# A hybrid encoder layer: the recurrence's first chunks take their product banks from the sweeps' and memory's set instead of the convolution's

## The chip, the cores and the metric

The kernel runs on one core of a Trainium2 chip. The metric is device time in microseconds (us) of one execution; the time before is the median of three runs. Engines: PE = TensorE, DVE = VectorE, ACT = ScalarE, POOL = GpSimd, SP = SyncE (here only a queue that issues DMAs).

## The reference

One encoder layer over 2048 rows of width 1024, fp32. What matters here:

```python
u = _rms_norm(h, norm_mix_g);  proj = u @ w_in
y_hy = _group_rms_norm(_hyena(...))            # convolution over the whole length, by rFFT
y_ml = _group_rms_norm(_mlstm_bidirectional(q, k, v, o_pre, gates, gate_b))  # 4 heads x 128
h = h + concatenate([y_hy, y_ml]) @ w_out
h = h + _cross_attention(_rms_norm(h), _rms_norm(mem), wq, wk, wv, wo)       # 256 memory rows
h = h + square(relu(_rms_norm(h) @ ff_w1)) @ ff_w2
```

The mLSTM is a linear recurrence with gates, computed chunk by chunk:

```python
s = einsum('bhtd,bhsd->bhts', qc, kc) * w                       # scores of the chunk
num = einsum('bhts,bhse->bhte', s, vc) + inter * einsum('bhtd,bhde->bhte', qc, C)
C_new = carry_decay * C + einsum('bhs,bhsd,bhse->bhde', we, kc, vc)
```

It runs forwards and backwards, and the two are summed.

## The kernel before

The kernel works through stages: the input projection ("sweeps"), the long convolution (`hyena`, in steps of PE products at L173 and L186), the gates and the backward states of the recurrence (`states`), a projection of the memory rows (`memproj`), the recurrence (`mlstm`, 16 chunks of 128 rows), the attention with its gemms (L355, L358, L359 are the three partial products of one fp32 product), and the feed-forward part. Neighbouring stages are written interleaved. A scheduler then sets the order of the instructions on each engine from its own estimate of when each can start; so where a tile lives, and what must be free before it can be written, changes the order.

PE writes its products into PSUM. PSUM is eight banks of 128 x 512 fp32 and is divided here in two sets of four: `mm()` gives a bank of the first set (sweeps, memory projection, attention gemms), `hy()` one of the second (convolution, states, recurrence, the attention's transposes). The names `mm<-` and `hy<-` in the rows of the profile tell the set. A bank is given again when everything that reads it is done.

`memproj` goes through eight groups: `project` (L708, 16 products with weights `wm`, then a copy on ACT at L710), and for each of them either `keys` (L725, 16 products in four banks, groups 0 to 3) or `values` (L737, 8 products in four banks, groups 4 to 7). Each bank is copied on ACT (L715) to a tile `o`, which a DMA issued by POOL (L727 `gd<-o`, L739 `vw<-o`) writes to memory.

One chunk of `mlstm` is, on PE: four products `kk_t` by `qn` into one bank (`scores`, L1284); for each of the two directions, eight products in two banks (L1322 from the scores and `va`, L1324 from the state `cf` forwards or `cbn` backwards); and four products in two banks for the new state (`update`, L1200). Chunk 0 has no forward state and so no L1324 in its first direction. Between them POOL and ACT prepare the weights `rw` (L1290, L1291, L1293), DVE multiplies them with the scores (L1294) and brings rows by shuffles (L1275), ACT or DVE divides and reads the two banks (L1327, L1330, L1331; forwards ACT at L1336, backwards DVE at L1338), and DVE forms the state (L1206). After each second chunk `bank_rsqrt` (L208 to L216) computes 13 small operations in one bank, DVE scales the rows (L1356), and a DMA of POOL writes them to `ym`. The scores of chunk n + 1 are written ahead of the products of chunk n.

A step of the convolution does its products into two banks, then L1051 (DVE), L1060 (POOL), L1062 (DVE), `bank_rsqrt` in a third bank, L1064 (DVE), L1066 (POOL), and four DMAs `yh<-a` (L1068). The attention begins by loading rows of `yh` (L1473), turning them on PE (`turn`, L1479) and splitting them (L366) for the first gemm L355.

SP's queue loads everything else: weights `wm` (L415), convolution operands `a<-zg` and `a<-hy` (L339, L974), and the chunks' `qn`, `kk_t`, `cbn`, `va`, `kn`, `og`.

The code around the change, in the program's order: `for _ in chain(p.turned_in(), take(n, 1), beside_each(n, take(m, 5))): pass`, where n is `memproj` and m is `mlstm`: one step of the memory projection, then the remaining steps and the first steps of the recurrence in turn.

Of the kernel before, what the change touches and what calls it, by code (L numbers as in the profile page):

```python
# [128 lines left out]
class Prog:  # L129
    def __init__(self, ctx, tc, a):  # L130
        self.tc, self.nc, self.a = tc, tc.nc, a
        nc = self.nc
        self.ctx = ctx
        self.dr = ctx.enter_context(tc.tile_pool(name="dr", bufs=1, space=DRAM))
        self.s = {}
        cp = self.cp = ctx.enter_context(tc.tile_pool(name="cp", bufs=1))
        ident = cp.tile([128, 128], F32, name="ident")
        nc.gpsimd.memset(ident, 1.0)
        nc.gpsimd.affine_select(ident, ident, pattern=[[-1, 128]], compare_op=ALU.is_equal, fill=0.0,
                                base=0, channel_multiplier=1)  # L140
        self.ident = ident
        self.eps = cp.tile([128, 1], F32, name="eps")
        nc.vector.memset(self.eps, EPS)
        self.ones = cp.tile([128, 128], F32, name="ones")
        nc.vector.memset(self.ones, 1.0)
        self.flip = 0
        self.banks, self.strict = [], False
        self.pending = []
        self.prepq = None
        self.hooks, self.made, self.lag, self.rowb = {}, 0, [], None  # L150
        self.rbp = cp.tile([128, 16], F32, name="rbp")
        self.fb = cp.tile([128, 8], F32, name="fb")
        nc.scalar.activation(self.fb[:, 4:5], self.eps, AF.Copy)
        par = self.par = cp.tile([128, 192], F32, name="par")
        nc.scalar.dma_start(out=par, in_=a["par"])
        self.g_mix, self.g_mem, self.gx, self.gf = (par[:, 8 * i:8 * i + 8] for i in range(4))
        self.cw = par[:, 32:92].rearrange("p (i c) -> p i c", i=3)
        self.cb, self.gb = par[:, 92:112], par[:, 112:128]
        self.ps = ctx.enter_context(tc.tile_pool(name="ps", bufs=1, space=PSUM))
# [4 lines left out]
    def hy(self):  # L164
        t = self.ps.tile([128, 512], F32, tag="hy", name="hy", bufs=4)
        self.banks.append(t[:, 0:1].tensor.name)
        return t

    def beside(self, *products, pin=False):
        names = [p[0].tensor.name for p in products]  # L170
# [31 lines left out]
        else:  # L202
            self.nc.vector.tensor_copy(out, in_)

    def bank_rsqrt(self, pool, ss, n):
        nc, c = self.nc, ss.shape[1]
        m, ys = (pool.tile([128, c], F32, tag="br" + x, name="br" + x, bufs=2) for x in "my")
        nc.scalar.activation(m, ss, AF.Identity, bias=self.eps, scale=1.0 / n)  # L208
        b = self.hy()
        y, t = b[:, 0:c], b[:, 16:16 + c]  # L210
        nc.vector.tensor_scalar(y.bitcast(I32), m.bitcast(I32), -0.5, float(0x5F3759DF), ALU.mult, ALU.add)
        for _ in range(3):
            nc.vector.tensor_copy(ys, y)
            nc.vector.tensor_tensor(t, y, ys, ALU.mult)
            nc.vector.scalar_tensor_tensor(t, t, -0.5, m, ALU.mult, ALU.mult)
            nc.vector.scalar_tensor_tensor(y, t, 1.5, ys, ALU.add, ALU.mult)  # L216
        return y
# [970 lines left out]
    def update(self, sb, new, old, kk, va, r, eng, pin=None, bufs=2):  # L1188
        nc, pin = self.nc, pin or (lambda i: i)
        WC, DC = self.gcols[:, 2], self.gcols[:, 3]  # L1190
        ve = sb.tile([128, 4, 129], F32, tag="ve", name="ve", bufs=bufs) if bufs > 1 else va
        if eng is nc.scalar:
            for h in range(4):
                eng.activation(ve[:, h], va[:, h], AF.Copy, scale=WC[:, r + h:r + h + 1])
        else:
            eng.tensor_tensor(ve, va, WC[:, r:r + 4].unsqueeze(2).broadcast_to([128, 4, 129]), ALU.mult)
        for p in range(2):
            pc = self.hy()
            for i in range(2):
                pin(nc.tensor.matmul(pc[:, 129 * i:129 * i + 129], kk[:, 2 * p + i], ve[:, 2 * p + i], start=True, stop=True))  # L1200
            if old is None:
                nc.vector.tensor_copy(new[:, 2 * p:2 * p + 2].rearrange("d h e -> d (h e)"), pc[:, 0:258])
                continue
            for i in range(2):
                h = 2 * p + i
                nc.vector.scalar_tensor_tensor(new[:, h], old[:, h], DC[:, r + h:r + h + 1],  # L1206
                                               pc[:, 129 * i:129 * i + 129], ALU.mult, ALU.add)
# [19 lines left out]
    def mlstm(self, es):  # L1227
# [51 lines left out]

        def scores(n, ld):  # L1280
            qn, kk_t, cbn, va, rows_ = ld
            sp = self.hy().rearrange("p (h t) -> p h t", h=4)
            for h in range(4):
                nc.tensor.matmul(sp[:, h], kk_t[:, h], qn[:, h], start=True, stop=True)  # L1284
            for d in range(2):
                r = 64 * d + 4 * n
                nm = rows_[d, 0]
                if (d, 1) in rows_:
                    it = rows_[d, 1]
                    nc.gpsimd.tensor_tensor(it, it, qn, ALU.mult)  # L1290
                nc.gpsimd.tensor_tensor(nm, nm, masks[d].unsqueeze(1).broadcast_to([128, 4, 128]), ALU.add)  # L1291
                for h in range(4):
                    nc.scalar.activation(nm[:, h], nm[:, h], AF.Exp, bias=GC[:, r + h:r + h + 1])  # L1293
                nc.vector.tensor_tensor(nm, nm, sp, ALU.mult)  # L1294
# [4 lines left out]
        for n in range(16):  # L1299
# [10 lines left out]
            for d in range(2):  # L1310
                r = 64 * d + 4 * n
                nm = rows_[d, 0]
                state = cf if d == 0 else cbn
                if d == 0:
                    y = sb.tile([128, 4, 128], F32, tag="h0", name="ht", bufs=2)
                pvs = []
                for p in range(2):
                    pn = self.hy()
                    for i in range(2):
                        h = 2 * p + i  # L1320
                        dst = pn[:, 129 * i:129 * i + 129]
                        nc.tensor.matmul(dst, nm[:, h], va[:, h], start=True, stop=state is None)  # L1322
                        if state is not None:
                            nc.tensor.matmul(dst, rows_[d, 1][:, h], state[:, h], start=False, stop=True)  # L1324
                    pvs.append(pn[:, 0:258].rearrange("t (h e) -> t h e", h=2))
                for p, pv in enumerate(pvs):
                    nc.scalar.activation(pn[:, 260 + 2 * p:262 + 2 * p].unsqueeze(2), pv[:, :, 128:129], AF.Abs)  # L1327
                den = sb.tile([128, 4, 1], F32, tag="den", name="den", bufs=4)
                dv = den.rearrange("t h o -> t (h o)")
                nc.vector.tensor_tensor(dv, pn[:, 260:264], EC[:, r:r + 4], ALU.max)  # L1330
                nc.vector.reciprocal(dv, dv)  # L1331
                for p, pv in enumerate(pvs):
                    for i in range(2):
                        h = 2 * p + i
                        if d == 0:
                            nc.scalar.activation(y[:, h], pv[:, i, 0:128], AF.Copy, scale=dv[:, h:h + 1])  # L1336
                            continue
                        nc.vector.scalar_tensor_tensor(y[:, h], pv[:, i, 0:128], dv[:, h:h + 1], y[:, h], ALU.mult, ALU.add)  # L1338
# [10 lines left out]
                nc.scalar.activation(junk[:, h], y[:, h], AF.Square, accum_out=ss[:, c:c + 1])  # L1349
            ys.append(y)  # L1350
            if n % 2:
                rv = self.bank_rsqrt(sb, ss, 128)
                for i, y in enumerate(ys):
                    t0 = 128 * (n - 1 + i)
                    for h in range(4):
                        nc.vector.scalar_tensor_tensor(y[:, h], y[:, h], rv[:, 4 * i + h:4 * i + h + 1],  # L1356
                                                       gml[:, 128 * h:128 * h + 128], ALU.mult, ALU.mult)
                    stores.append(lambda t0=t0, y=y: nc.gpsimd.dma_start(
                        out=ym[t0:t0 + 128].rearrange("t (h e) -> t h e", h=4), in_=y))
# [717 lines left out]
def chain(*gens):  # L2077
    for g in gens:
        yield from g
# [20 lines left out]
def program(p):  # L2100
    with ExitStack() as ms:
        with ExitStack() as es:
# [13 lines left out]
            n = p.memproj()  # L2116
            m = p.mlstm(ms)
            with ExitStack() as hs:
# [4 lines left out]
                             among(chain(p.sweep((6, 7), 0, False), p.natural(0, (2,), p.prep_mem, 2)), back, 1),  # L2123
                             )
                weave(rest, p.hyena(hs), 445, 329)
            for _ in chain(p.turned_in(), take(n, 1), beside_each(n, take(m, 5))):
                pass
        with ExitStack() as rs:
            p.ts = rs.enter_context(ExitStack())
            p.tail_open(p.ts)  # L2130
# [71 lines left out]
```

## Time and profile before

| what | value |
|---|---|
| time, median of 3 runs | 3063.18 us (3056.71 to 3065.72) |
| time of the profiled execution | 3063.97 us |
| its span, first to last instruction | 3062.3 us |
| mean granted TensorE clock | 0.989 |
| PE busy | 97% of the span |
| memory projection's last product ends, first attention product L355 starts | 1131.7 us, 1170.91 us |

In the profile's views "x8" counts records, of which PE leaves two for most products; an idle time in square brackets is what the engine waited just before the row, with the instruction or transfer that ended it. "PEclk" is the granted clock as a share of full speed, and the DMA share is the mean busy share of the core's 16 DMA engines.

### The profile page before, as it was taken

The numbers are of one execution on the slowest core, as the hardware profiler recorded it, in microseconds if no ns is written. First come the engines' busy times: TensorE is split into PE (matmuls) and PEld (weight loads), VectorE is DVE, ScalarE is ACT, GpSimd is POOL, SyncE is SP. The second block draws the span as 40 slices with busy tenths as digits, with TensorE's granted clock in tenths as the row PEclk, the third lists the DMA queues.
The fourth block names the chain that finished last, engine by engine and source line by source line (L and its number), as shares of the span: only waits on it lengthen the run. The fifth ranks groups of instructions, "written<-read, shape, count | busy, mean of one in ns | idle before, by whom it ended". The sixth has DMA issues, their size and how long they took to land.

```text
span 3062.3 us, 44144 instructions
## 1 busy us (share of the span) xinstructions
PE 2979.0 (97%) x14799; PEld 2367.6 (77%) x14799; DVE 1953.2 (64%) x3442; ACT 1491.5 (49%) x2930; POOL 1263.4 (41%) x1025
## 2 busy tenths in 40 slices
PE   9999999998999989999999999999999999999998
PEld 7666667775678867888888888888888888888876
DVE  8855464557755447867665666558555686566695
ACT  6443455634664235555544455556555543333335
POOL 0112113321443654333223247765665374344653
PEclk9999999999999999999999999999999999999999
DMA  6655676686877976463567466657544555444434
GB/s 223 197 186 170 213 263 214 192 273 216 279 229 221 348 265 198 149 228 125 196 202 264 137 219 217 208 178 250 190 151 152 196 192 169 118 157 121 155 103 165
DMA packets 423644, 607.03 MB, mean 198 GB/s; under 512 B 36847, under 2 KB 229999, under 8 KB 422393
## 3 DMA queue, kind: packets, MB, share of 16 engines
q1 hardware_dynamic: 395972, 525.42, 53.6%
q0 software_dynamic: 18992, 62.96, 5.6%
q10 hardware_dynamic: 8452, 15.83, 1.4%
q8 instruction: 117, 1.92, 0.3%
q14 instruction: 111, 0.90, 0.1%
HBM read 401.67 MB, written 202.41 MB: 197 GB/s over the span
## 4 chain that ended last, share of the span: by engine, by line
PE 58%; DVE 2%; DMA 1%; issue 1%; ACT 1%; POOL 0%; SPq 0%; DVEq 0%; POOLq 0%; ACTq 0%
PE mm L355 12%; PE mm L359 12%; PE mm L358 12%; PE hy L355 6%; PE hy L359 6%; PE hy L358 6%; PE hy L1322 1%; PE hy L1324 1%; DVE bl L1693 0%; PE hy L1284 0%; PE hy L1596 0%; DVE acc L1991 0%; PE hy L1200 0%; PE hy L1479 0%; DVE acc L2028 0%
## 5 line engine op out<-in xcount | busy, mean ns | idle before, releaser
L1692 ACT CAST ah<-w 128x512 fp32r<-128x512 f32 x284 | 176.6, 623 | 303.8 <-PE hy L358 150.2
L1693 DVE TENSOR_TENSOR bl<-wr,bh 128x512 fp32r<-128x512 f32 x213 | 240.3, 1132 | 126.5 <-ACT bh L1692 126.2
L366 DVE TENSOR_TENSOR wl<-wn,wh 128x512 fp32r<-128x512 f32 (+1 forms) x296 | 220.0, 787 | 89.2 <-ACT wh L366 89.2
L355 PE MATMUL mm<-xh,wh 128*128 128x512 f32 x640 | 264.5, 415 | 2.3 <-ACT xh L366 1.1
L358 PE MATMUL mm<-xl,wh 128*128 128x512 f32 x640 | 255.9, 400 | 5.5 <-DVE xl L366 5.4
L359 PE MATMUL mm<-xh,wl 128*128 128x512 f32 x640 | 254.5, 398 | 0.0
L1692 ACT CAST bh<-wr 128x512 fp32r<-128x512 f32 x232 | 143.4, 621 | 227.9 <-PE mm L359 169.5
L1693 DVE TENSOR_TENSOR al<-w,ah 128x512 fp32r<-128x512 f32 x236 | 216.5, 918 | 57.2 <-ACT ah L1692 56.9
L359 PE MATMUL mm<-bh,al 128*128 128x512 f32 x576 | 223.8, 391 | 3.4 <-DVE al L1693 3.4
L355 PE MATMUL mm<-bh,ah 128*128 128x512 f32 x576 | 225.9, 392 | 1.3 <-DVE acc L1854 1.1
L358 PE MATMUL mm<-bl,ah 128*128 128x512 f32 x576 | 224.9, 390 | 0.0
L366 ACT CAST wh<-wn 128x512 fp32r<-128x512 f32 (+1 forms) x296 | 164.3, 620 | 102.6 <-PE mm L359 51.1
L358 PE MATMUL mm<-act,wh 128*128 128x512 f32 x512 | 202.0, 395 | 0.0
L359 PE MATMUL mm<-act,wl 128*128 128x512 f32 x512 | 199.9, 392 | 0.0
L355 PE MATMUL mm<-act,wh 128*128 128x512 f32 x512 | 199.0, 395 | 0.6 <-ACT wh L366 0.5
L355 PE MATMUL hy<-bh,ah 128*128 128x512 f32 x448 | 175.2, 391 | 0.0
L358 PE MATMUL hy<-bl,ah 128*128 128x512 f32 x448 | 174.6, 390 | 0.0
L359 PE MATMUL hy<-bh,al 128*128 128x512 f32 x448 | 174.4, 390 | 0.0
L331 POOL TENSOR_TENSOR b<-b 128x512 f32<-128x512 f32 x32 | 48.1, 1504 | 293.6 <-DVE b L330 277.4
L355 PEld LDWEIGHTS mm<-xh,wh 128*128 128x128 f32 x640 | 121.1, 190 | 52.4 <-issue 18.7
L358 PEld LDWEIGHTS mm<-xl,wh 128*128 128x128 f32 x640 | 121.2, 189 | 50.9 <-issue 19.1
L355 PE MATMUL mm<-wh,xh 128*128 128x256 f32 (+1 forms) x512 | 155.7, 304 | 1.8 <-DVE a L960 1.8
(396 smaller groups left out, 8257.4 us busy)
## 6 DMA issues: line engine op xcount, KB each, us to landing
wr<-hc SPq DMA_DIRECT2D x224, 256.0 KB
w<-in_ff_w_dram SPq DMA_DIRECT2D x172, 256.0 KB
hc<-wn SPq DMA_DIRECT2D x128, 256.0 KB
wn<-in_w_in_dram SPq DMA_DIRECT2D x100, 256.0 KB
hc<-q SPq DMA_DIRECT2D x96, 256.0 KB
fs<-a SPq DMA_DIRECT2D x32, 512.0 KB
zs<-a POOLq DMA_DIRECT2D x32, 512.0 KB, 6.6
a<-fs SPq DMA_DIRECT2D x64, 256.0 KB
```

Source lines behind the costliest of these rows:

```text
L331: nc.gpsimd.tensor_tensor(b, f, b, ALU.subtract)
L355: first = mm(ps, lh, rh, start=start, stop=False)
L358: mm(ps, lh, rl, start=False, stop=False)
L359: self.last = mm(ps, ll, rh, start=False, stop=stop)
L366: both = (self.nc.scalar.copy(hi, src), self.nc.vector.tensor_tensor(lo, src, hi.bitcast(F32), ALU.subtract))
L1322: nc.tensor.matmul(dst, nm[:, h], va[:, h], start=True, stop=state is None)
L1324: nc.tensor.matmul(dst, rows_[d, 1][:, h], state[:, h], start=False, stop=True)
L1692: self.nc.scalar.copy(hi, src)
L1693: eng.tensor_tensor(lo, src, hi.bitcast(F32), ALU.subtract)
```

## The change

A method `spare()` gives a bank of the first set while a flag `early` is set, and of the second otherwise. Scores, chunk products, the state's product and the bank of the chunk's `bank_rsqrt` call it. The flag is set only around the loop in which the memory projection and the first chunks of the recurrence are written. Chunks written later, beside the attention, take `hy()` as before; so do the backward states and the convolution, which are written earlier.

```diff
+        self.early = False
...
+    def spare(self):
+        return self.mm() if self.early else self.hy()
...
-    def bank_rsqrt(self, pool, ss, n):
+    def bank_rsqrt(self, pool, ss, n, bank=None):
...
-        b = self.hy()
+        b = bank or self.hy()
...
         for p in range(2):                       # update
-            pc = self.hy()
+            pc = self.spare()
...
-            sp = self.hy().rearrange("p (h t) -> p h t", h=4)
+            sp = self.spare().rearrange("p (h t) -> p h t", h=4)
...
                 for p in range(2):               # a chunk's direction
-                    pn = self.hy()
+                    pn = self.spare()
...
-                rv = self.bank_rsqrt(sb, ss, 128)
+                rv = self.bank_rsqrt(sb, ss, 128, self.spare())
...
+            p.early = True
             for _ in chain(p.turned_in(), take(n, 1), beside_each(n, take(m, 5))):
                 pass
+            p.early = False
```

Both kernels issue the same number of instructions on every engine. The order differs on PE between about 1024 and 1184 us of the profile, and on the other engines in the same place; before and behind it the two orders are the same. In the rows below a number such as x16 counts instructions. The line numbers of the changed kernel are four higher than the profile's from L177 on (L1288 is L1284, L1326 and L1328 are L1322 and L1324, L1204 is L1200, L712 is L708, L729 is L725, L741 is L737, L1483 is L1479, L359 is L355, L177 and L190 are L173 and L186).

On PE in the kernel before, the end of the memory projection: the last products of its values groups, then chunk 2 (first rows only).

```order
L1324 MATMUL hy<-cbn,rw 128x129
L737 MATMUL mm<-wm,kt 128x512 x3
L1200 MATMUL hy<-ve,kn 128x129 x4
L1284 MATMUL hy<-qn,kk_t 128x128 x4
L1322 MATMUL hy<-va,rw 128x129
L1324 MATMUL hy<-cf,rw 128x129
```

Behind these rows come the rest of chunk 2, the whole of chunk 3, the 16 transposes of L1479, half a direction of chunk 4 and then the first L355, with no other product between.

On PE in the changed kernel, the same end.

```order
L1204 MATMUL mm<-ve,kn 128x129 x4
L712 MATMUL mm<-mt,wm 128x256 x16
L741 MATMUL mm<-wm,kt 128x512 x8
L712 MATMUL mm<-mt,wm 128x256 x16
L741 MATMUL mm<-wm,kt 128x512 x16
L1483 MATMUL hy<-ident,wn 128x128 x16
L1288 MATMUL hy<-qn,kk_t 128x128 x4
L1326 MATMUL hy<-va,rw 128x129
L1328 MATMUL hy<-cf,rw 128x129
```

The first row is the end of chunk 3; after it the last three groups of the projection stand without a chunk between, and the transposes and chunk 4 follow the last L741 at once.

On PE in the changed kernel, chunk 0 and the convolution steps around it, in the second and third group of the keys.

```order
L729 MATMUL mm<-kt,wm 128x256 x12
L1288 MATMUL mm<-qn,kk_t 128x128 x4
L1326 MATMUL mm<-va,rw 128x129 x5
L1204 MATMUL hy<-va,kn 128x129 x4
L1326 MATMUL mm<-va,rw 128x129
L1204 MATMUL mm<-ve,kn 128x129 x4
L712 MATMUL mm<-mt,wm 128x256 x13
L177 MATMUL hy<-a,e_2743 32x512
L190 MATMUL hy<-a,e_2743 32x512 x7
L712 MATMUL mm<-mt,wm 128x256 x3
```

Before, at this place stood only L708, L725 and convolution steps; chunk 0's L1284 came behind the last convolution step. Row 4 is a backward state of the recurrence, which keeps its `hy` bank.

On PE in the changed kernel, the last two convolution steps, after the products of chunk 1.

```order
L1328 MATMUL mm<-cbn,rw 128x129
L177 MATMUL hy<-a,e_2743 32x512
L190 MATMUL hy<-a,e_2743 32x512 x7
L1204 MATMUL mm<-ve,kn 128x129 x4
L177 MATMUL hy<-a,e_2743 32x512
L190 MATMUL hy<-a,e_2743 32x512 x7
L712 MATMUL mm<-mt,wm 128x256 x16
```

Before, at least 19 products of L708 and L725 or L737 lay between two steps of the convolution; here four L1204 lie between the last two.

## The prediction

> **What bounds the kernel now.** I read the page's busy table first, then the windows around the code that the change touches, then PE's own timeline there, then the timelines of DVE and SP. The page:
>
> ```profile
> PE 2979.0 (97%) x14799; PEld 2367.6 (77%) x14799; DVE 1953.2 (64%) x3442; ACT 1491.5 (49%) x2930; POOL 1263.4 (41%) x1025
> ```
>
> PE sets the time: 97% busy, so only what changes PE's own idle or slow time can move the end. The change adds and removes no instruction; it moves rows of about 1024 to 1184 us. These windows (length, busy time of PE, PEld, DVE, ACT, POOL, then granted clock, DMA share, GB/s) show that piece:
>
> ```profile
> 1025.00:1045.00 20.00, 20.00 (x109) 16.74 (x108) 9.88 (x31) 3.72 (x7) 11.05 (x13) 1.00 1.04 386
> 1065.00:1085.00 20.00, 20.00 (x91) 14.19 (x91) 11.33 (x33) 4.61 (x9) 15.12 (x19) 1.00 1.04 353
> 1085.00:1105.00 20.00, 20.00 (x90) 13.16 (x89) 6.07 (x17) 4.30 (x8) 12.40 (x15) 1.00 0.83 315
> 1105.00:1131.50 26.50, 26.50 (x132) 18.43 (x131) 13.72 (x38) 14.13 (x49) 15.09 (x18) 1.00 0.71 222
> 1131.50:1171.00 39.50, 23.39 (x138) 21.39 (x136) 26.16 (x98) 22.64 (x88) 19.23 (x18) 0.74 0.58 186
> ```
>
> Up to 1131.5 (the memory projection) PE is full at full clock, with the DMA engines full too until 1085. The last row, a tail between the memory projection and the first attention product, is the slow place: PE is idle for 16 of 39.5 us and the clock is 0.74. PE's timeline there (start, duration, instructions in a row, then the idle time before them and what ended it):
>
> ```profile
> 1128.97 2.74 PE L737 MATMUL mm<-wm,kt 128*128 128x512 f32 x6
> 1134.20 1.13 PE L1284 MATMUL hy<-qn,kk_t 128*128 128x128 f32 x8 [1.60 <-issue]
> 1142.23 0.77 PE L1322 MATMUL hy<-va,rw 128*128 128x129 f32 x2 [5.12 <-DVE bry L213]
> 1145.10 0.80 PE L1322 MATMUL hy<-va,rw 128*128 128x129 f32 x2 [0.81 <-DVE ht L1356]
> 1149.31 2.09 PE L1200 MATMUL hy<-ve,kn 128*128 128x129 f32 x8 [2.12 <-ACT ht L1336]
> 1151.19 1.92 PE L1284 MATMUL hy<-qn,kk_t 128*128 128x128 f32 x8
> 1156.51 0.39 PE L1322 MATMUL hy<-va,rw 128*128 128x129 f32 x2
> 1156.73 0.39 PE L1324 MATMUL hy<-cbn,rw 128*128 128x129 f32 x2
> 1157.48 1.23 PE L1200 MATMUL hy<-ve,kn 128*128 128x129 f32 x8 [0.36 <-ACT ht L1336]
> 1159.41 0.66 PE L1479 MATMUL hy<-ident,wn 128*128 128x128 f32 x4 [0.70 <-DVE cf L1206]
> 1160.38 1.29 PE L1479 MATMUL hy<-ident,wn 128*128 128x128 f32 x8 [0.32 <-issue]
> 1166.72 1.12 PE L1479 MATMUL hy<-ident,wn 128*128 128x128 f32 x4 [5.04 <-DVE act L366]
> 1170.91 1.18 PE L355 MATMUL mm<-act,wh 128*128 128x512 f32 x4
> ```
>
> L1284, L1322/L1324 and L1200 are one chunk of the recurrence. Chunks 2 and 3 run here alone: each step waits for DVE or ACT, with no other product between. The idle times add up to 16.07 us. The same instructions take twice as long after a wait (L1284 1.92 against 1.05 at full clock, row below; L1200 2.09 against 1.06), so part of the busy time is lost too.
>
> **What the change does to it.** The pieces of order above show it: chunks 0 to 3 move from the end of the memory projection to between its product groups (chunk 0 behind keys 1, chunk 1 behind keys 2, chunk 2 behind keys 3, chunk 3 behind values 0), since a score or a chunk product no longer waits for a convolution bank. After the last L737 follow the transposes of L1479, chunk 4 and L355.
>
> Count from 1024.22, where the first row differs, to the first L355 at 1170.91: 146.7 us. PE's work between is the same in both kernels. These are rows for its rates:
>
> ```profile
> 1020.70 3.68 PE L725 MATMUL mm<-kt,wm 128*128 128x256 f32 x8 [2.36 <-ACT kt L710]
> 1024.22 4.91 PE L708 MATMUL mm<-mt,wm 128*128 128x256 f32 x22
> 1047.94 1.89 PE L725 MATMUL mm<-kt,wm 128*128 128x256 f32 x8
> 1063.07 0.61 PE L173 MATMUL hy<-a,e 64*32 64x512 f32 x1
> 1073.35 0.61 PE L173 MATMUL hy<-a,e 64*32 64x512 f32 x1
> 1086.18 0.61 PE L173 MATMUL hy<-a,e 64*32 64x512 f32 x1
> 1121.93 1.05 PE L1284 MATMUL hy<-qn,kk_t 128*128 128x128 f32 x8
> 1131.54 1.06 PE L1200 MATMUL hy<-ve,kn 128*128 128x129 f32 x8
> ```
>
> Removed, first term. The tail holds three groups each of L1284 and L1200 (0.9 us from start to start at full clock), 36 products of L1322/L1324 (0.22 apart, as at 1156.51 and 1156.73) and 16 of L1479 (0.16): 5.4 + 8.0 + 2.6 = 16.0 us at full rate. It takes 39.4, of which 16.1 are idle, so 7.3 are lost to the clock. Full-rate work from 1024.22 is 146.7 - 16.1 - 7.3 = 123.3 us: if the new order never waited, the gain would be 23.4 us.
>
> Added, second term: what stays bare at the end. In before, the load of the hyena rows for L1479 waits for the last L737 (it takes over memory of the weights) and hides under chunks 2 and 3:
>
> ```profile
> 1131.77 0.81 SPq L1473 DMA_DIRECT2D wn<-yh  x2
> ym<-ht POOLq DMA_DIRECT2D x2, 256.0 KB, 2.3
> gd<-o POOLq DMA_DIRECT2D x16, 256.0 KB, 7.5
> ```
>
> Its rule stays, and now nothing stands between. The trace does not show this load's own landing; the landings beside it run from 2.3 to 7.5 us. I take 3, near the lower, as the projection's transfers are over by then. The 5.04 wait of the fourth transpose should go: it was for DVE's splits, queued behind a chunk's normalisation, which will be past. Bounds: 2 to 10 with that wait back.
>
> Added, third term: waits inside the projection. A chunk holds two banks for a direction's products until ACT (L1336) or DVE (L1338) has read them, and one bank for its scores. All of these now come from the same four banks that L708, L725 and L737 need, so a chunk can hold up projection products and the other way round. These DVE rows price one convolution step between two products (L1051 to L1064), which runs on the same engine in order:
>
> ```profile
> 1064.19 1.29 DVE L1051 TENSOR_TENSOR a<-hy,a 128x512 f32<-128x512 f32 x2 [4.41 <-PE hy L186]
> 1067.49 1.22 DVE L1062 TENSOR_REDUCE ms<-a 128x16 f32<-128x1024 f32 x1 [2.01 <-POOL a L1060]
> 1071.87 1.22 DVE L1064 TENSOR_TENSOR a<-a,hy 128x1024 f32<-128x1024 f32 x1
> 1144.97 0.72 DVE L1275 STREAM_SHUFFLE rw<-rows 128x512 f32<-128x512 f32 x1
> 1149.04 1.13 DVE L1338 SCALAR_TENSOR_TENSOR ht<-hy,den,ht 128x128 f32<-128x128 f32 x4 [0.55 <-ACT ht L1336]
> 1153.21 1.29 DVE L1294 TENSOR_TENSOR rw<-rw,hy 128x512 f32<-128x512 f32 x2 [1.17 <-PE hy L1284]
> ```
>
> - Chunk 0 (third piece of order): its second direction waits until the first one's two banks are read, which needs L1330, L1331 and four L1336 behind DVE's convolution reduce of 1.22. As L1200 waits 2.12 for ht in the tail, I take 4.2 for three such waits of 0.6 to 2.1. Bounds 0 and 6.4.
> - Chunk 1: its L1200 waits for ht as in the tail, 2.12 and one L1336 more: 3.0.
> - The last convolution steps. L173 in before stands 10.3 and 12.8 us apart (rows above). In the new order the last three have only chunk 1 and 0.9 us of L1200 between. The last needs the bank that L1064 of two steps before gives free: a step is 8.9 us on DVE (1064.19 to 1073.09), and four shuffles of 0.7, an L1294 pair of 1.29 and an L1338 of 1.13 stand among it, 14.1 in all. PE has meanwhile four L725 (0.9), L1284 and L1200 (0.9 each), 16 products (3.6) and one step (1.0), 7.3: it waits 6.8 us. Bounds 0 and 10.
> - Chunks 2 and 3: behind keys 3 and values 0 each waits for copies (ACT L715) of the group before, and for ht: some seven waits of 0.4 to 2, 6.5 us together. A wait gives the engines behind it the same time, so I count half, 3.3.
>
> Together 17.3, between 0 and 27.
>
> Fourth term: after a wait the clock may drop. The row at 1020.70 shows the price: 2.36 idle, then 3.68 for work that takes 1.89 at 1047.94, a loss of 1.8. Two of the waits above are longer than 2.36, so 3.6; bounds 0 and 7.3, the tail's own loss. The Trainium skill ("TensorE: Matmul & The Clock Gate", A second HAM failure mode: psum-queue depth-cycling) says that short idle times between product groups that cycle through PSUM banks can make the clock swing between half and full. By that rule the clock would fall at every chunk (rival three below); this trace shows one such fall after a single wait of 2.36, and none in the windows quoted from 1025 to 1131.5, where no wait shows.
>
> Sum: -23.4 + 3.0 + 17.3 + 3.6 = +0.5 us. Behind the first L355 the order is word for word the old one and PE-bound, so a shift carries to the end one for one. Costed at nothing: the same copies and DMA issues in another order on ACT and POOL, covered by PE as long as POOL (15.12 busy of 20 at 1065) keeps up; if that cover goes, the copies L715 come late, which is in the third term's upper bound. The profiled execution took 3063.97 us (span 3062.3 and 1.7 around it); the median of the runs is 3063.18, 0.8 less. I forecast 3063.97 + 0.5 = 3064.5, or 3063.7 beside the median: no change that shows. The measurement tells about 0.3% (9.2 us) from nothing.
>
> **Rivals.** One, the projection has room: third and fourth terms near 2 and 0, as in before, where chunks 0 and 1 run between the last L737 groups with no wait shown (window 1105 to 1131.5, PE 26.50 of 26.50). Then -23.4 + 3.0 + 2 = -18, 3045 us. For it: DVE and ACT are half idle there. Against it: chunks 0 and 1 have eight banks now, and the new order gives them the four that the projection uses.
>
> Two, slower: the DMA engines decide. The rows for it, of the DMA view, SP and PE:
>
> ```profile
> qn<-qt SPq DMA_DIRECT2D x8, 256.0 KB
> cbn<-cbd SPq DMA_DIRECT2D x6, 258.0 KB
> 1086.28 8.94 SPq L415 DMA_DIRECT2D wm<-in_xa_wo_dram  x4
> 1109.77 1.02 PE L737 MATMUL mm<-wm,kt 128*128 128x512 f32 x2
> ```
>
> A chunk loads about 1.5 MB (qn, kk_t, kn, va, og of 256 KB each and cbn), and 7 MB of five chunks must now land before some 1110, where before most came later. The engines are full (1.04) until 1085; at 353 GB/s 7 MB are 20 us. The last weights are issued by 1095.2; with a landing of 7.5 they are there 7 us before the L737 at 1109.77. As soon as the added transfers delay them by more, L708 and L737 wait: 20 - 7 = 13 us more, on top of the waits counted: 3064 + 13 = 3077 us. For it: the full windows. Against: 1085 to 1131 has 0.71 to 0.83, and the projection itself becomes longer by the chunks' 12 us.
>
> Three, slower: the clock falls at each of the four chunks. A chunk is 5.4 us of PE (0.9 + 16 x 0.22 + 0.9); at half rate 4 x 5.4 = 21.6 in place of 3.6: 3082 us.
>
> Four, the change does nothing: the order excludes it.
>
> **How the numbers follow.** Forecast (within 9 us of no change) 0.42; rival one, faster, 0.35; rival two 0.17; rival three 0.06. Faster by over 0.3%: 0.35; within: 0.42; slower: 0.23. The range reaches to rival one and to rival two: 3044 to 3080; the forecast alone is 3055 to 3072.
>
> **What would show it.** Right: the first L355 within 9 us of 1170.9; after the last L737 less than 10 us to it instead of 39; waits of L1284, L1322, L1200 and L173 for ACT o, ACT ht and DVE L1064 inside the projection, 12 to 20 us in sum; a clock under 1.00 in two windows there. Wrong: a full PE through the projection (rival one), waits of L708 or L737 for wm (rival two), or a clock of 0.7 over the whole stretch (rival three).

## The result, and the profile after

The changed kernel takes 3079.69 us (median of 6, 3075.47 to 3082.99) against 3064.45 us of the kernel before on the same chips: ratio 1.0053, interval 1.0042 to 1.0065, slower by 0.5%. The profiled execution took 3076.4 us (span 3074.7), 12.4 more than the one of before. I had forecast no change at 3063.7, and the time lies at the upper end of the range.

The first attention product starts at 1182.47 instead of 1170.91, and the difference of 11.6 stays to the end (12.4). The windows of the changed kernel, with the same columns as those of before:

```profile
1025.00:1045.00 20.00, 15.21 (x95) 12.50 (x94) 7.73 (x19) 4.25 (x11) 11.92 (x14) 0.98 1.06 362
1065.00:1085.00 20.00, 11.50 (x88) 8.27 (x88) 14.71 (x49) 6.67 (x28) 16.87 (x17) 0.84 1.05 348
1085.00:1105.00 20.00, 16.75 (x75) 12.72 (x76) 14.96 (x50) 6.45 (x23) 13.71 (x18) 0.84 0.48 140
1145.00:1165.00 20.00, 18.84 (x60) 11.13 (x59) 1.79 (x7) 4.68 (x8) 6.13 (x9) 1.00 0.34 137
```

The projection, where PE was full at full clock, now has the holes: PE is busy for 11.5 of 20 us from 1065, at a clock of 0.84. From 1085 the DMA share falls to 0.48: between 1074.3 and 1106.8 SP issues only two loads of weights (at 1095.26), and of that time it waits 9.1 us for PE's L712 and 10.5 for L729. In the last window PE is busy again, for 18.84 of 20 us at full clock; the 0.34 there is the end of the loads, as the projection's last weights were issued at 1142.28. PE's timeline, the rows with the longest waits and the end:

```profile
1020.04 1.05 PE L1288 MATMUL mm<-qn,kk_t 128*128 128x128 f32 x8
1044.95 0.80 PE L1326 MATMUL mm<-va,rw 128*128 128x129 f32 x2 [4.22 <-DVE hy L218]
1048.12 1.23 PE L1204 MATMUL mm<-ve,kn 128*128 128x129 f32 x4 [1.42 <-ACT o L719]
1074.15 0.49 PE L1326 MATMUL mm<-va,rw 128*128 128x129 f32 x2 [3.55 <-ACT o L719]
1085.50 1.03 PE L177 MATMUL hy<-a,e 64*32 64x512 f32 x1 [5.42 <-issue]
1087.39 7.84 PE L712 MATMUL mm<-mt,wm 128*128 128x256 f32 x32
1101.44 5.41 PE L729 MATMUL mm<-kt,wm 128*128 128x256 f32 x16 [2.75 <-DVE ht L1360]
1146.85 3.70 PE L741 MATMUL mm<-wm,kt 128*128 128x512 f32 x8 [1.17 <-DVE ht L1360]
1157.29 13.90 PE L741 MATMUL mm<-wm,kt 128*128 128x512 f32 x32
1174.36 1.09 PE L1483 MATMUL hy<-ident,wn 128*128 128x128 f32 x4 [3.17 <-DMA wn<-yh]
1178.90 1.91 PE L1288 MATMUL hy<-qn,kk_t 128*128 128x128 f32 x8
1182.47 1.17 PE L359 MATMUL mm<-act,wh 128*128 128x512 f32 x4
```

The tail is gone as the order said: 11.3 us from the last L741 (ends 1171.2) to the first attention product, where it was 39.2. In its place come waits in the projection, 22.0 us in sum, and half-rate time behind the longer ones. None of these waits is for weights `wm`.

What stands behind three of them is seen in the timelines of SP, POOL, DVE and ACT. For the 4.22 (first five rows), for the 3.55 (the next three) and for the 5.42 (the last):

```profile
1028.99 0.38 SPq L1263 DMA_DIRECT2D qn<-qt  x1
...
1038.76 1.27 POOL L1294 TENSOR_TENSOR rw<-rw,qn 128x512 f32<-128x512 f32 x1 [6.50 <-DMA qn<-qt]
1040.80 1.91 POOL L1064 TENSOR_TENSOR a<-a 128x1024 f32<-128x1024 f32 x1
...
1042.74 1.22 DVE L1066 TENSOR_REDUCE ms<-a 128x16 f32<-128x1024 f32 x1 [2.85 <-POOL a L1064]
...
1044.28 1.14 ACT L1340 ACTIVATE ht<-mm,den 128x128 f32<-128x128 f32 x4
...
1064.51 0.53 SPq L1188 DMA_DIRECT2D va<-vd  x1
...
1073.23 0.40 ACT L1198 ACTIVATE ve<-va,cols 128x129 f32<-128x129 f32 x1 [5.07 <-DMA va<-vd]
1073.53 0.56 ACT L719 COPY o<-mm 128x512 f32<-128x512 f32 x1
...
1084.18 1.22 DVE L1068 TENSOR_TENSOR a<-a,hy 128x1024 f32<-128x1024 f32 x1
```

A chunk's `qn` is issued at 1028.99, and POOL, which needs it next in its line, waits until 1038.76. The convolution's L1064 stands behind it on POOL, the reduce L1066 behind that on DVE, chunk 0's denominator behind the reduce, and ACT reads chunk 0's two banks at 1044.28 only. In the second case a load of `va` takes 8.7 us, ACT waits for it with the copy of a projection bank next in its line, and PE waits for that bank. The page's releaser names what ended just before (L218, L719), not the load. In the third case DVE's L1068, which reads a bank of the convolution's set, ends at 1085.40, and PE's next convolution step starts at 1085.50.

### The profile page after: what moved, and what is told of

It reads as the page before. It is cut to its first block, busy times and chain, and to the rows that moved or that the text cites. A ratio compares the mean times of both kernels' runs of the same rounds, so it can differ in the third digit from the quotient of the medians.

```text
span 3074.7 us, 44127 instructions
## 1 busy us (share of the span) xinstructions
PE 2981.8 (97%) x14799; PEld 2365.6 (77%) x14799; DVE 1939.2 (63%) x3442; ACT 1491.8 (49%) x2930; POOL 1262.9 (41%) x1025
## 4 chain that ended last, share of the span: by engine, by line
PE 79%; issue 6%; DVE 6%; DMA 6%; POOL 2%; ACT 1%; SPq 1%; DVEq 0%; POOLq 0%; ACTq 0%
PE mm L359 16%; PE mm L362 16%; PE mm L363 16%; PE hy L359 6%; PE hy L363 6%; PE hy L362 6%; PE mm L960 2%; PE hy L1034 2%; PE hy L991 2%; PE hy L177 1%; PE mm L712 1%; PE hy L1326 1%; PE hy L1328 1%; PE hy L1204 1%; PE mm L741 1%
## 5 line engine op out<-in xcount | busy, mean ns | idle before, releaser
L359 PE MATMUL mm<-xh,wh 128*128 128x512 f32 x640 | 263.8, 414 | 3.1 <-ACT xh L370 1.6
L359 PE MATMUL mm<-bh,ah 128*128 128x512 f32 x576 | 226.2, 393 | 1.0 <-DVE acc L1858 0.9
L359 PE MATMUL mm<-act,wh 128*128 128x512 f32 x512 | 199.1, 395 | 1.9 <-ACT wh L370 1.8
L359 PE MATMUL hy<-bh,ah 128*128 128x512 f32 x448 | 175.2, 391 | 0.0
L359 PEld LDWEIGHTS mm<-xh,wh 128*128 128x128 f32 x640 | 120.3, 188 | 52.7 <-issue 19.8
L359 PE MATMUL mm<-wh,xh 128*128 128x256 f32 (+1 forms) x512 | 155.2, 303 | 1.8 <-DVE a L964 1.8
```

What stands on the lines that cost most here:

```text
L359: first = mm(ps, lh, rh, start=start, stop=False)
```

## The experiments

Times are medians, ratios are to the kernel before in the same comparison. "Stretch" is from the convolution step near 1010 us to the first attention product in the profiled execution (before 160.8), "idle" PE's waits in it (before 18.4). The profiled execution can be longer than the median: by 7.0 us in root_back, 6.4 in no_load_wait, 5.6 in scores_products and scores_late.

| kernel | time us | ratio (interval) | stretch, idle |
|---|---|---|---|
| changed | 3079.69 | 1.0053 (1.0042 to 1.0065) | 174.0, 27.3 |
| late2 | 3075.97 | 1.0037 (1.0022 to 1.0053) | 175.4, 27.6 |
| late3 | 3069.08 | 1.0015 (1.0005 to 1.0025) | 168.7, 23.8 |
| late4 | 3069.07 | 1.0016 (1.0001 to 1.0031) | 160.5, 18.4 |
| only_scores | 3053.04 | 0.9967 (0.9954 to 0.9979) | 151.7, 13.1 |
| scores_again | 3055.03 | 0.9983 (0.9973 to 0.9994) | 156.2, 14.7 |
| scores_late | 3058.18 | 0.9988 (0.9979 to 0.9997) | 157.3, 17.8 |
| scores_state | 3058.34 | 0.9996 (0.9985 to 1.0006) | 161.2, 18.8 |
| scores_products | 3079.74 | 1.0060 (1.0047 to 1.0073) | 185.4, 34.7 |
| root_back | 3079.51 | 1.0059 (1.0038 to 1.0079) | 179.2, 33.1 |
| no_load_wait | 3072.65 | 1.0030 (1.0018 to 1.0042) | 177.1, 31.4 |
| filled | 3080.65 | 1.0056 (1.0038 to 1.0075) | 176.9, 23.1 |
| before_filled | 3061.53 | 0.9996 (0.9985 to 1.0006) | 157.6, 13.4 |
| all_deeper_loads | 3090.02 | 1.0094 (1.0080 to 1.0107) | not comparable |
| scores_deeper_loads | 3066.95 | 1.0019 (1.0008 to 1.0029) | not comparable |

**Where the chunks stand.** late2, late3 and late4 write the first chunk one, two or three projection groups later, with all banks as in the change:

```diff
-            for _ in chain(p.turned_in(), take(n, 1), beside_each(n, take(m, 5))):
+            for _ in chain(p.turned_in(), take(n, 2), beside_each(n, take(m, 5))):   # late2; 3 late3; 4 late4
```

> The changed kernel, with the first chunk written one group of the memory projection later. In its order chunk 0 stands behind keys 2 and chunk 1 behind keys 3, each with one or two convolution steps inside; chunks 2 and 3 behind values 0 and 1; no two convolution steps stand close together. Theory A (the time is lost where a chunk meets the convolution's steps on DVE, ACT and POOL): the 5.4 us wait between the last two convolution steps goes, with its half-rate time, the other waits halve: some 14 us of idle and 6 of clock loss between the first row that differs and the first attention product, 144 us against 162, so 3061 to 3068 us. Theory B (the four shared banks themselves: each chunk and each product group wait for one another wherever they stand): 20 us of idle or more, 3075 to 3082.

> The changed kernel, with the first chunk written two groups later. Chunk 0 stands behind keys 3 with one convolution step inside, chunks 1 to 3 behind values 0, 1 and 2, past the last convolution step but one, and 8 products of values 3 are left for the end. Theory A: only chunk 0 meets the convolution; some 8 us of idle inside the projection, 4 in the tail, 5 of clock loss: 140 us, so 3054 to 3062 us, faster than before. Theory B: 3075 to 3082.

> The changed kernel, with the first chunk written three groups later. All chunks stand behind the last convolution step, chunks 0 to 2 behind values 0 to 2, chunk 3 after the last product of the projection, beside the transposes. Theory A: some 6 us of idle inside the projection, 6 to 8 in the tail around chunk 3, 5 of clock loss: 142 us, so 3055 to 3063 us. Theory B: the same waits as in the changed kernel less those of one chunk, 3072 to 3080.

The loss falls with the distance from the convolution, 0.53, 0.37, 0.15, 0.16%, though the intervals of the first two overlap, and no version is faster than before. late2 came out as theory B said (3076 us, 27.6 of idle); late3 and late4 lie between the two theories. So theory A gives the direction and not the size, and theory B (the same loss everywhere) doesn't hold for the last two. In late4 no chunk product stands among the convolution's steps on PE, and still one wait of 8.2 us stands in chunk 0 (rows of PE, SP, POOL and ACT):

```profile
1091.94 1.90 PE L1326 MATMUL mm<-va,rw 128*128 128x129 f32 x6 [8.19 <-ACT o L719]
...
1075.38 0.38 SPq L1263 DMA_DIRECT2D qn<-qt  x1
...
1084.32 1.26 POOL L1294 TENSOR_TENSOR rw<-rw,qn 128x512 f32<-128x512 f32 x1 [8.38 <-DMA qn<-qt]
1085.53 0.79 POOL L731 DMA_DIRECT2D gd<-o  x1
1086.32 1.47 POOL L743 DMA_DIRECT2D vw<-o  x2
...
1091.31 0.59 ACT L719 COPY o<-mm 128x512 f32<-128x512 f32 x1 [12.87 <-DMA gd<-o]
```

POOL waits 8.4 us for `qn`; the stores of the projection that it should issue come behind; ACT has no free tile `o` and can't copy; PE has no bank. This is theory C, which I formed from these rows. Late4 also shows that the start of the attention isn't all: its first attention product is 4.2 us earlier than before, but chunk 3 moves into the attention, which then waits 2.3 us for L1360 and 3.6 for `ym` rows, where before had no wait, and the span is 2.8 us longer.

**Which bank.** Four kinds of banks are moved. Each of these gives some of them back to `hy()`:

```diff
 only_scores, scores_again: pn, pc and the root's bank   = self.hy()
 scores_late:               as only_scores, and take(n, 3)
 scores_state:              pn and the root's bank       = self.hy()
 scores_products:           pc and the root's bank       = self.hy()
 root_back:                 the root's bank              = self.hy()
```

> Only the scores take the projection's banks; chunk products, the state's products and the bank of the reciprocal root stay with the convolution's. In its order the scores come early as in the changed kernel, but the chunk products stand behind the last convolution step. Theory A: no product of a chunk meets the convolution; a score holds one bank of the projection for long (until DVE's multiplication), a few waits of 1 to 3 us: 3055 to 3066 us. Theory B: with three banks left to the projection for long stretches, more waits there, 3070 to 3080.

> Scores and the state's products take the projection's banks, the chunk products and the reciprocal root the convolution's. Chunk products stand behind the last convolution step but one, between the values groups. Theory (the chunk products in the projection's banks, two held until ACT or DVE has read them, are what costs, and late chunk products are cheap): as with the scores alone or a little better, 3048 to 3057 us. Rival (any further bank taken from the projection costs as much): 3062 to 3075.

> Scores and chunk products take the projection's banks; the state's products and the reciprocal root stay with the convolution's. It completes the set: scores alone 0.9967 of before, scores and state 0.9996, all but the root 1.0059, all 1.0053. Theory (the chunk products in these banks let the scheduler put chunks among the convolution steps, and that costs): 3077 to 3084 us. Rival (state's products or the sum of all banks taken): 3056 to 3070.

> The changed kernel with the bank of the chunks' reciprocal root given by the convolution's set again; scores and products stay with the projection's. PE's order differs only around the last convolution step. Theory: the waits of L729 and L741 for the normalisation of two chunks (2.8 and 1.2 us, and about 2 of half rate) go: 3073 to 3077 us. Rival (DVE's line is late by that much in any case, and the wait moves on): 3078 to 3083.

This set is the clearest answer. Scores alone: 0.9967, better than I expected, and 0.9983 when run again. With the state's products: 0.9996, between my theory and its rival. With the chunk products instead: 1.0060, as slow as with everything. Giving back only the root's bank: 1.0059, no better, as the rival said; in its profile the waits for L1360 are gone and another of 14.0 us, for ACT's L1340 behind a late store of `ym`, has come:

```profile
1122.40 2.09 PE L1204 MATMUL mm<-ve,kn 128*128 128x129 f32 x8 [14.00 <-ACT ht L1340]
```

scores_products and only_scores differ in the chunk products' banks alone, so these banks carry the loss. While the products need a convolution bank, the scheduler puts them behind the last convolution step (the first L1326 of only_scores is at 1088.66); in a projection bank they go among the convolution steps and the fullest DMA time (1037.75 in the changed kernel, 1038.24 in scores_products). The scores come early in all of them: their preparation is done when the products start, and in only_scores the tail is filled too. PE in only_scores:

```profile
1088.66 1.28 PE L1326 MATMUL hy<-va,rw 128*128 128x129 f32 x10
1096.03 0.80 PE L1326 MATMUL hy<-va,rw 128*128 128x129 f32 x2 [5.42 <-ACT ht L1340]
1105.44 1.13 PE L1288 MATMUL mm<-qn,kk_t 128*128 128x128 f32 x8 [1.45 <-DMA qn<-qt]
1148.00 3.60 PE L741 MATMUL mm<-wm,kt 128*128 128x512 f32 x8
1154.70 2.16 PE L1483 MATMUL hy<-ident,wn 128*128 128x128 f32 x8 [3.11 <-DMA wn<-yh]
1161.29 1.17 PE L359 MATMUL mm<-act,wh 128*128 128x512 f32 x4
```

Beside a wait of 2.35 near 1020, which stands in before too, two waits of weight (5.42 and 1.45) and the bare load are all that is left; the first attention product starts 9.6 us before that of the kernel before, and the span is 9.4 shorter. scores_late speaks for the filled tail as the gain: with the same banks but chunk 3 behind the last projection product again, it has 9.2 us of idle in its tail and gains 0.12%, about as the theory below said. Its interval overlaps that of scores_again, so this is not shown.

> The kernel with only the scores in the projection's banks, once more in more rounds, since it is the one version that came out faster than before. If the first measurement (0.9967 of before) holds: 3049 to 3056 us beside a before of 3062; if it was the chip or the day: within 0.2% of before.

> As with only the scores in the projection's banks, but the first chunk is written two groups later; in PE's order chunk 3 then stands behind the last product of the projection again, followed by the transposes, as chunk 3 does in the kernel before. Theory (the gain of the scores alone is the tail that it fills): half of the gain goes, 3056 to 3062 us, with 5 to 9 us of idle behind the last projection product. Rival (it is the earlier scores themselves): 3050 to 3055.

The version with only the scores beats both kernels in both measurements. The second, 0.17% faster with an interval of 0.06 to 0.27, fits either expectation above (3055.03 us, and within 0.2% of before); I take the gain as 0.17 to 0.33%.

**The late loads.** In the changed kernel two operations of the early chunks are given constants instead of loaded tiles, for chunks 0 to 3:

```diff
-                    nc.gpsimd.tensor_tensor(it, it, qn, ALU.mult)
+                    nc.gpsimd.tensor_tensor(it, it, <a constant tile> if self.early else qn, ALU.mult)
-                eng.activation(ve[:, h], va[:, h], AF.Copy, ...)
+                eng.activation(ve[:, h], <a constant tile> if self.early else va[:, h], AF.Copy, ...)
```

> The changed kernel, with two operations of chunks 0 to 3 reading constants in place of freshly loaded tiles: POOL's product of the rows with qn (L1294 of the changed kernel) and ACT's scaling of va (L1198). It leaves out these two factors of the recurrence in those chunks; all loads stay, and PE still reads qn and va. PE's order is the changed kernel's but for some products' places. Theory C (a chunk's loads take 9 us to land while the DMA engines are full, POOL and ACT stand still before them, and stores, copies and convolution steps queued behind them hold PE's banks): the waits of 4.2, 1.4, 3.6 and 5.4 us fall to some 6 us together, the clock loss by some 4: 3065 to 3071 us. Rival (the banks are held by the chain of products, copies and DVE anyway): 3076 to 3083.

The loss falls from 0.53 to 0.30%; the time, 3072.65 us, lies between theory C and its rival. ACT's waits for `va` from 1010 to 1165 us (total, times, longest), in the changed kernel:

```profile
ACT ve L1198 <- DMA va<-vd: 29.1, 6, 9.1
```

and in this one:

```profile
ACT ve L1198 <- DMA va<-vd: 5.7, 1, 5.7
```

In the kernel before it is 11.1 us. The waits of chunk 0 fall from 6.2 to 2.7 us; the 5.4 before the last convolution step is still 4.7, so the two loads are not what sets that one. In the profiled execution PE waits 11.1 us for another load of a chunk:

```profile
1062.55 0.80 PE L1328 MATMUL mm<-cbn,rw 128*128 128x129 f32 x2 [11.09 <-DMA cbn<-cbd]
```

So late loads are a part of the loss: some 7 us of 15 by the medians, and anything from 2 to 12 if the two intervals are taken as independent. The rest, DVE's line and the banks by the rows above, is argued and not measured apart. A late load need not cost time: in only_scores, which is faster than before, POOL still waits 5.7 us for `qn` and ACT 16.0 for `va`.

Two kernels give `qn` and `kk_t` a third buffer (`bufs=3` in `loads`), the first beside the whole change, the second beside the scores alone.

> The changed kernel with three in place of two buffers for qn and kk_t, so that a chunk's loads can be issued one chunk earlier. The scheduler sets another order: chunk 0 behind keys 2, the chunks' products still among the last convolution steps and in the projection's banks. Theory C (late loads hold POOL and ACT): the waits for copies and for ht halve, 3063 to 3071 us. Rival (banks and DVE's line): 3075 to 3083.

> Only the scores in the projection's banks, and three buffers for qn and kk_t. In its order the chunk products stand between the values groups, 13 products of L737 behind the last chunk. Theory C: the waits for POOL and ACT fall, and the tail is filled: 3044 to 3052 us. Rival: the same as with the scores alone, 3052 to 3057.

Both are slower, and neither tests what it was made for. The first chunk's loads come later, not earlier, probably because the wider buffers find room only when other memory comes free (SP of the second kernel; in only_scores this `qn` is issued at 1005.17):

```profile
1026.77 0.46 SPq L419 DMA_DIRECT2D wm<-in_xa_wq_t_dram  x1
1037.38 0.38 SPq L1262 DMA_DIRECT2D qn<-qt  x1
```

Convolution steps were moved together too, and PE waits 10.2 us for one and 7.4 for `kk_t` in the first kernel, 12.0 and 6.2 in the second. They are inconclusive on theory C.

**The clock.** Spare products are put into an unused corner of a bank that is held anyway:

```diff
+                    if n < 2 and p == 1 and d == 0:        # filled, on the change: 14 for each of chunks 0 and 1
+                    if n == 2 and d == 0 and p == 1:       # before_filled, on the kernel before: 18
+                        for _ in range(...):
+                            nc.tensor.matmul(pn[:, 384:512], kk_t[:, 0], qn[:, 0], start=True, stop=True)
```

> The changed kernel with 28 spare products (128x128, 0.22 us each, 6.2 us in all) in an unused corner of a bank that is held anyway, behind the first direction of chunks 0 and 1, where PE waited 4.2 and 3.6 us. They compute nothing that is used. Theory (the half-rate time behind the waits is a large part of the loss): the two waits shrink by what the spare products take, and the clock does not fall behind them, so PE's work behind them runs 3 to 4 us faster: 3073 to 3079 us though PE has 6.2 us more to do. Rival (idle time alone matters): 3080 to 3086.

> The kernel before, with 18 spare products (0.22 us each, 4.0 us) in an unused corner of a bank of chunk 2, between its two directions, where PE waits 5.1 us for the reciprocal root and then runs at half rate for some 11 us. They compute nothing that is used; the order is otherwise the old one. Theory (the half rate comes from the idle time before it): the wait falls to some 1 us, the products behind it run at full rate, the first attention product starts 3 to 5 us earlier: 3057 to 3060 us. Rival (the clock falls for another reason, or the chain on DVE sets the end anyway): within 2 us of before.

filled has 6.2 us more PE work and takes as long as the changed kernel, which is the lower end of the rival's range: its idle is 4.2 us less, its busy time 7.1 more. The half rate behind the first filled wait is gone, but other waits (3.4 and 3.8 us) have it. before_filled, which came out as its rival said, shows why filling this one wait is worth nothing (the first row is the last scores ahead of the wait with the spare products):

```profile
1133.73 4.18 PE L1328 MATMUL hy<-qn,kk_t 128*128 128x128 f32 x36
1139.01 0.46 PE L1322 MATMUL hy<-va,rw 128*128 128x129 f32 x2 [1.10 <-DVE bry L213]
1141.88 0.80 PE L1322 MATMUL hy<-va,rw 128*128 128x129 f32 x2 [1.74 <-DVE ht L1359]
1146.89 2.09 PE L1200 MATMUL hy<-ve,kn 128*128 128x129 f32 x8 [2.92 <-ACT ht L1339]
```

The wait for `bry` falls from 5.12 to 1.10, and the products behind it run at full rate (0.46, where it was 0.77). So here the idle time before is what halves the clock. But the next waits grow from 0.81 to 1.74 and from 2.12 to 2.92, since DVE and ACT are no earlier: from the last L737 to the first attention product it takes 38.8 us, as before (39.2), and the time is the same within the interval. Where a chain over other engines sets the end, half-rate products fill time that would be waited for.

## Why the prediction was wrong

Its direction of each term was right and its sum was not. From the first differing row to the first attention product it took 162.4 us (1020.04 to 1182.47) against 146.7, that is +15.7, where I had +0.5. The first differing row came 4.2 us earlier in this execution than in that of before (1.7 were there at the convolution step near 1010 already, the rest is a shorter wait and a clock that did not fall at 1020); so the first attention product moved by 11.6 only. Three of the four signs of a right forecast were missed, two of them narrowly: the first attention product is 11.6 us late and not at most 9, it takes 11.3 us from the last L741 and not less than 10, and the waits are 22.0 us and not 12 to 20. Term by term:

- **Removed, -23.4.** The tail's idle is 3.8 us instead of 16.1, as the order said. As an account of time it held. But before_filled shows, for one of the waits, that clock loss in the tail could not have been won by itself.
- **Bare end, +3.0.** Measured 3.17 and 0.61, so 3.8. The 5.04 wait of the fourth transpose went, as forecast.
- **Waits in the projection, +17.3.** Measured 22.0. Chunk 0: 4.2 forecast, 0.6 + 4.2 + 1.4 = 6.2 measured, near the bound. Chunk 1's L1200 had no wait for ht, but its second direction one of 3.55 for a copy. The convolution step: 6.8 forecast, 5.4 measured, by the L1064 named (L1068 of the changed kernel; the page says "issue"). My sum had a slip there: four L725 take 1.8 us (1.89 for eight records), not 0.9, so the wait comes out at 5.9. Behind it 2.75, 0.36, 0.35, 0.80, 1.37 and 1.17, 6.8 in all, near the 6.5 that I had worked out and then halved because a wait would give the engines behind it time. That the 6.5 fits is partly luck: only 0.80 and 0.36 are for copies and for ht, as I had said; 2.75 and 1.17 are for L1360 in the root's bank, which I had not counted among the banks that a chunk takes, and 0.35 and 1.37 for the state.
- **Clock, +3.6, bounds 0 and 7.3.** This is the step that failed: the term was sized at 3.6 us and measured 12.5, beyond its upper bound. 162.4 us less 25.8 idle is 136.7; the full-rate work is 123.3 and 0.9 for four more products of chunk 4 ahead of L355, so 12.5 us went to the clock; the granted clock was 0.84 in the windows from 1065 to 1105. I had counted two falls of 1.8, for waits longer than 2.36, where the clock fell behind more waits and stayed down longer. The rows show it fall behind 4.22 and 1.42, behind 3.55 and 5.42, behind 2.75 and behind 3.17, and stay down for more than one row each time (L712 takes 7.84 instead of 7.17 after the 5.42, the L729 at 1101.44 5.41 instead of 3.62). Nor is 2.36 a limit. The same four products near 1020, which took 3.68 us behind the 2.36 in before, run at full rate behind as long a wait in only_scores and a longer one in scores_state (one row of each), and the runs don't show what decides it:

```profile
1020.17 1.99 PE L729 MATMUL mm<-kt,wm 128*128 128x256 f32 x8 [2.35 <-ACT kt L714]
...
1017.66 1.99 PE L729 MATMUL mm<-kt,wm 128*128 128x256 f32 x8 [2.59 <-ACT kt L714]
```

With these, -23.4 + 3.8 + 22.0 + 12.5 + 0.9 = +15.8: 8.9 of the 15.3 missed are the clock, 4.7 the waits, 1.7 the rest.

The rule of the Trainium skill that I set beside the fourth term ("TensorE: Matmul & The Clock Gate", A second HAM failure mode: psum-queue depth-cycling) was nearer than my count, with four falls instead of two. But the clock did not fall at every chunk: chunks 2 and 3 ran at full rate, behind waits of 0.35 to 1.37, and so the 21.6 of rival three was too high.

Of the rivals, the first (room in the projection) is refuted by the rows: 22 us of waits. The second had a part of the cause, at the wrong place: the DMA engines are full, but no projection product waits for weights. From the issue of a chunk's own loads to their first reader it takes 8.7 and 9.8 us in the rows above, and POOL and ACT, which serve the convolution and the projection in the same line, stand still for them. I had these loads in view only as a weight of 7 MB, and I had put the new order on ACT and POOL at nothing, as covered by PE; the waits of PE for L719 and behind L1064 show that the cover was gone.

Open remain the share of the late loads against DVE's line and the banks (one experiment, 2 to 12 of 15 us), what makes the clock fall behind one wait and not behind another of the same length, and whether an earlier place for the loads would win it, since a third buffer moved them the wrong way.

## What to carry to other kernels

A pool that gives work more banks also tells the scheduler that this work may start earlier; ask at which place it will then stand, and what its first operations on the in-order engines wait for there. Count idle time of PE with its clock: in the stretch of the twelve comparable kernels without spare products the half-rate loss (the stretch less its idle and its 133 to 136 us of full-rate work) was 0.34 to 0.51 us for each us of idle (before 9.1 to 18.4, changed 12.6 to 27.3, scores alone 4.5 to 13.1). And move the part whose results are wanted early (here one bank of scores), not all that can be moved: in the profiled executions it took 9.1 and 4.5 us out of the same stage in which the whole change lost 13.2.

## What the runs showed of the hardware

Eight L1360 on DVE, which read two tiles from SBUF, take 2.21 to 2.23 us where POOL computes nothing beside them, 3.24 to 3.29 beside one operation of POOL of 1.3 to 1.4 us, and 4.87 beside L1070 and L1064. Three cases of the changed kernel:

```profile
1144.57 2.22 DVE L1360 SCALAR_TENSOR_TENSOR ht<-ht,mm,gml 128x128 f32<-128x128 f32 x8
...
1288.29 3.29 DVE L1360 SCALAR_TENSOR_TENSOR ht<-ht,hy,gml 128x128 f32<-128x128 f32 x8
1288.54 1.28 POOL L1295 TENSOR_TENSOR rw<-rw,mask 128x512 f32<-128x512 f32 x1 [10.62 <-DVE rw L1279]
...
1096.52 4.87 DVE L1360 SCALAR_TENSOR_TENSOR ht<-ht,mm,gml 128x128 f32<-128x128 f32 x8
1095.39 2.61 POOL L1070 TENSOR_TENSOR a<-a,ghy 128x512 f32<-128x512 f32 x2 [4.90 <-DVE bry L217]
1097.96 1.94 POOL L1064 TENSOR_TENSOR a<-a 128x1024 f32<-128x1024 f32 x1
```

In root_back it is 4.83 beside L1070. The 4.87 ends at 1101.39, just as the 2.75 wait of L729 does; with 2.22 in its place that wait could have been 2.65 shorter. The Trainium skill ("SBUF — State Buffer", Who interferes with whom) says that a DVE instruction with two SBUF inputs contends with a GpSimd instruction that reads SBUF, and calls the ports that the two share an exclusive lock; the rows agree with it. I had not costed it: no such pair meets in the kernel before in the stretch that I read, though four of its eight groups of L1356 further on take 3.26 to 3.29 us.
